# Router logits with the padded weights stationary: one change to a hybrid attention and mixture-of-experts block

## The chip, the cores and the metric

The kernel runs on one core of a Trainium2 chip. The metric is the device time of one execution in microseconds (us); the kernel before was timed three times. Engines: PE is TensorE's matmul, PEld its weight load, DVE VectorE, ACT ScalarE, POOL GpSimd, SP SyncE, which here only issues DMAs. Each engine works through its own instructions in order.

## The reference

One decoder block on 512 tokens of width 1024, all float32. The part that the change touches comes after attention:

```python
x = x + (gate_p * pool_out + gate_a * attn_out) @ w_out[l]
hn = rmsnorm(x, norm2_g[l]).reshape(B * S, D)
x = x + hier_moe(hn, w_router_group[l], b_router_group[l], ...)
# inside hier_moe
pg = softmax(hn @ w_rg + b_rg)          # 4 groups, the best one is taken
le = hn @ w_re + b_re                   # 32 experts, 8 in each group
# top 2 of the chosen group's 8 experts; every token goes through those two
```

The router's logits are thus 36 numbers for each token: 4 group logits and 32 expert logits, a contraction over 1024 channels. All 32 experts have tokens, and each has three float32 matrices of 2 MB (gate, up, down).

## The kernel before, in words

The 512 tokens are four tiles of 128 (NT = 4). The first third computes the input projection, pooling, attention and the branch projections. Then `out_proj` (L777) multiplies the merged branches by w_out, chooses experts and gathers the rows of the first pair of experts; then a loop over 16 pairs of experts (L1087) does their gate, up and down projections and adds the results to the tokens. The schedule is written out by hand: the order of the instructions of each engine is the order in which the program issues them.

**The order in `out_proj`.** `tok_unit` (L266) issues 12 matmuls for one tile, half the channels and 512 output columns; `mid` names functions that it calls after its inner steps k = 0 to 3. After each unit `tick()` (L450) runs the tasks that `after(n, ...)` (L460) has set for then, in the order in which they were set. The second half of the columns takes eight units in the order (0,0) (1,0) (0,1) (2,0) (1,1) (3,0) (2,1) (3,1), each pair being (tile, half of the channels). When a tile's second unit is done, `x2_half` (L648) adds the residual on DVE (L650) and sums squares on ACT (L653), and `x2_rstd` (L655) makes the mean on DVE (L658, L659) and its inverse root on POOL. Tiles 0 and 1 then go on so: in the next unit the second half of the tile is transposed (`rt_transpose`, PE L680, copied out by ACT L681); after that unit come `norm2` (ACT L670), `store_rows` (a DMA from POOL's queue, L673), `rt_logits` (PE L690) and `rt_select` (twelve DVE instructions, L695 to L726, that end with the choice `A_b`); after the unit behind it comes `ranked` (L771), which counts on PE how many earlier tokens chose each expert (L739, L740) and makes R1 and P on DVE. Tile 2 does its logits inside the last unit. Tile 3 does them behind it, between the matmuls (L850) that gather the first pair's rows.

**The logits.** For each tile and each of 8 blocks of 128 channels, the transposed tokens are the stationary operand (128 x 128) and the router weights `wr` (128 x 36) move. A float32 matmul counts as two matmul instructions in the trace, so a tile's logits are 16.

**Buffers and loads.** Weights come through a pool of 23 buffers of 8 KB a partition (NBIG = 23), and so do the activations. `prefetch` (L614) puts loads of expert weights into SP's queue. A load waits there until its buffer is free, and the loads behind it wait too.

Of the kernel before, what the change touches and what calls it, by code (L numbers as in the profile page):

```python
# [10 lines left out]
F32 = mybir.dt.float32  # L11
# [6 lines left out]
OP = mybir.AluOpType  # L18
# [4 lines left out]
NT, ND = SEQ // 128, D // 128  # L23
# [3 lines left out]
NG, EPG, NE = 4, 8, 32  # L27
DE = 512
CAP = 64
# [19 lines left out]
def hybrid_block_kernel(  # L49
# [27 lines left out]
    nc = tc.nc  # L77
# [5 lines left out]
    const = ctx.enter_context(tc.tile_pool(name="const", bufs=1))  # L83
# [12 lines left out]
    def T(name="t"):  # L96
        return sm.tile([128, 512], F32, tag="T", name=f"{name}{next(names)}")
# [90 lines left out]
    lam_v = T("lam_v")[:, :4 * HD].rearrange("p (i d) -> p i d", i=4)  # L188
    cols = const.tile([128, 8], F32, name="cols")
    wgrp = T("wgrp")[:, :512].rearrange("p (g d) -> p g d", g=4)  # L190
    wr = const.tile([128, ND, NG + NE], F32, name="wr")
    br = const.tile([128, NG + NE], F32, name="br")

    for i, g in enumerate((q_norm_g, k_norm_g)):
# [8 lines left out]
    nc.sync.dma_start(cols[:, 4:5], bass.AP(tensor=subln_g.tensor, offset=subln_g.offset, ap=[[1, 128], [1, 1]]))  # L203
    nc.sync.dma_start(wgrp, pool_w[0].rearrange("g c d -> c g d"))
    nc.sync.dma_start(wr[:, :, :NG], w_rg[0].rearrange("(c p) n -> p c n", p=128))
    nc.sync.dma_start(wr[:, :, NG:], w_re[0].rearrange("(c p) n -> p c n", p=128))
    g2c = const.tile([128, ND], F32, name="g2c")
    g2p = const.tile([128, ND], F32, name="g2p")
    nc.sync.dma_start(g2p, bass.AP(tensor=norm2_g.tensor, offset=norm2_g.offset, ap=[[ND, 128], [1, ND]]))
# [14 lines left out]
    def late_consts():  # L224
        for h in range(H):
            ts(bias4[:, h, :], dist, -(2.0 ** (-8.0 * (h + 1) / H)), None, op0=OP.mult)
        nc.vector.reciprocal(rc, rc)
        nc.vector.tensor_copy(ident_h, ident)
        tt(wr, wr, g2c[:, :, None].to_broadcast([128, ND, NG + NE]), op=OP.mult)
        ts(qk_g[:, 0:1], qk_g[:, 0:1], HD ** -0.5, None, op0=OP.mult)  # L230
        ts(cols[:, 4:5], cols[:, 4:5], 1.0 - LAM_INIT, None, op0=OP.mult)
        lsum = const.tile([128, 2], F32, name="lsum")
        lscr = T("lscr")[:, :HD]
        for i in range(2):
            stt(lscr, lam_v[:, 2 * i, :], 1.0, lam_v[:, 2 * i + 1, :], op0=OP.mult, op1=OP.mult,
                accum_out=lsum[:, i:i + 1])
        nc.scalar.activation(lsum, lsum, AF.Exp)
        stt(neglam, lsum[:, 1:2], -LAM_INIT, lsum[:, 0:1], op0=OP.add, op1=OP.subtract)
# [221 lines left out]
    def after(n, fn):  # L460
        tasks.append((unit_no[0] + n, fn))
# [183 lines left out]
    sel = {}  # L645
# [20 lines left out]
    def norm2(t):  # L666

        if t == 0:
            xn2.extend(S([128, 2, ND, 128], name="xn2") for _ in range(2))
        nc.scalar.mul(xn2_tile(t), acc_t(t).rearrange("p (q j) -> p j q", j=ND), sel[t]["r"])  # L670
# [4 lines left out]
    def rt_transpose(t, hf):  # L675
        sel[t]["T", hf] = T("xgT")[:, :512].rearrange("p (j q) -> p j q", j=4)
        p = bank("th", (128, 4, 128))
        for j in range(4):
            c = hf * 4 + j
            nc.tensor.transpose(p[:, j, :], acc_t(t)[:, c * 128:(c + 1) * 128], ident)  # L680
        nc.scalar.copy(sel[t]["T", hf], p)  # L681

    def rt_logits(t, *halves):
        if t in (0, NT - 1) and 0 in halves:
            first["lg", t] = bank("lg", (128, NT, 128))
        q = sel[t]
        q["lg"] = first["lg", NT - 1 if t == NT - 1 else 0][:, t]
        for hf in halves:
            for j in range(4 * hf, 4 * hf + 4):
                mm(q["lg"][:, :NG + NE], q["T", hf][:, j % 4, :], wr[:, j, :], start=j == 0, stop=j == ND - 1)  # L690

    def select_ops(t):
        q = sel[t]
        lg = small([128, NG + NE], "lg", bufs=4)
        stt(lg, q["lg"][:, :NG + NE], q["r"], br, op0=OP.mult, op1=OP.add)  # L695
        yield
        mg = small([128, 1], "mg", bufs=4)
        nc.vector.tensor_reduce(mg, lg[:, :NG], axis=AX.X, op=OP.max)
        yield
        cand = small([128, NG], "cand")  # L700
        best = small([128, 1], "best")
        stt(cand, lg[:, :NG], mg, iota_g, op0=OP.is_equal, op1=OP.mult)
        yield
        nc.vector.tensor_reduce(best, cand, axis=AX.X, op=OP.max)
        yield
        pen = small([128, NG], "pen")
        ts(pen, iota_g, best, NEG, op0=OP.not_equal, op1=OP.mult)
        yield
        le = small([128, NG, EPG], "le", bufs=4)
        tt(le, lg[:, NG:].rearrange("p (g e) -> p g e", e=EPG), pen[:, :, None].to_broadcast([128, NG, EPG]),  # L710
           op=OP.add)
        yield
        le = le.rearrange("p g e -> p (g e)")
        top = small([128, 8], "top", bufs=4)
        nc.vector.max(top, le)
        yield
        idx = small([128, 8], "idx", U32)
        nc.vector.max_index(idx, top, le)
        yield
        idf = small([128, 2], "idf", bufs=4)  # L720
        nc.vector.tensor_copy(idf, idx[:, 0:2])
        yield
        o1 = small([128, NE], "o1", bufs=4)
        ts(o1, iota_u, idf[:, 0:1], None, op0=OP.is_equal)
        yield
        stt(A_b[:, t, :], iota_u, idf[:, 1:2], o1, op0=OP.is_equal, op1=OP.add)  # L726
        yield
        q["v"] = (lg, le, mg, top, idf, o1)

    def rt_select(t, n=None):  # L730
        if "ops" not in sel[t]:
            sel[t]["ops"] = select_ops(t)
        for _ in itertools.islice(sel[t]["ops"], n):
            pass

    def rt_rank(t):
        rk = sel[t]["lg"][:, 64:64 + NE]
        for s in range(t):
            mm(rk, ones_b, A_b[:, s, :], start=s == 0, stop=False)  # L739
        mm(rk, tri, A_b[:, t, :], start=t == 0, stop=True)  # L740
        stt(R1[:, t, :], rk, 1.0, A_b[:, t, :], op0=OP.add, op1=OP.mult)
# [35 lines left out]
    def out_proj():  # L777
        i = N_GEMM
        bs = [bank("wo") for _ in range(NT)]
        prefetch(PF[0])  # L780
        for kq in range(2):
            for t in range(NT):
                tok_unit(bs[t], i + kq, kq, t, merged, kq == 0, kq == 1)
                if kq == 1:
                    x2_half(t, 0, bs[t])
                    after(2, lambda t=t: rt_transpose(t, 0))
                tick()
        prefetch(PF[1])
        last = NT - 1
        bs = {}  # L790
        mid = {}
        for n, (t, kq) in enumerate(OUT_ORDER):
            if kq == 0:
                bs[t] = bank("wo")
            tok_unit(bs[t], i + 2 + kq, kq, t, merged, kq == 0, kq == 1, mid)
            mid = {}
            if kq == 1:
                x2_half(t, 1, bs[t])
                if t == last:
                    rt_select(last - 1, 5)  # L800
                x2_rstd(t)
                if t < last - 1:
                    mid = {1: lambda t=t: rt_transpose(t, 1)}
                    after(2, lambda t=t: norm2(t))
                    after(2, lambda t=t: store_rows(t))
                    after(2, lambda t=t: rt_logits(t, 0, 1))
                    after(2, lambda t=t: rt_select(t))
                    after(3, lambda t=t: ranked(t))
                elif t < last:
                    mid = {0: lambda t=t: rt_transpose(t, 1), 1: lambda t=t: rt_logits(t, 0),  # L810
                           2: lambda t=t: (norm2(t), rt_logits(t, 1), rt_select(t, 3))}
            tick()
        prefetch(PF[2])
        assert not tasks, tasks
        rt_logits(last, 0)
        rt_transpose(last, 1)
        gather_first(0, (0,))
        rt_logits(last, 1)
        rt_select(last - 1)
        ranked(last - 1)  # L820
        norm2(last)
        store_rows(last - 1)
        gather_first(0, (1,))
        gather_first(1)
        rt_select(last)
        prefetch(PF[3])
        first["io"] = S([128, 2, D], name="io")
        gather_first(last - 1)
        ranked(last)
        gather_first(last)  # L830
        store_rows(last)
        prefetch(1)
        pairs[0] = first
        for t in range(NT):
            rt_weights(t)
# [7 lines left out]
    def gather_first(t, parts=(0, 1)):  # L843

        if t == 0 and 0 in parts:
            first["b"] = [bank("xg", (128, 4, 128)) for _ in range(2)]
        for i in parts:
            b = first["b"][i]
            for j in range(4):
                mm(b[:, j, :], xn2_tile(t)[:, i * 4 + j, :], first["P"][:, t].rearrange("p e s -> p (e s)"),  # L850
                   start=t + j == 0, stop=t == NT - 1 and j == 3)
        if t == NT - 1:
            first["x"] = x_of(first["b"])
# [327 lines left out]
```

## Time and profile before

| what | value |
|---|---|
| time, median of 3 runs (lowest to highest) | 800.28 us (798.57 to 801.16) |
| the profiled execution: its time, its span | 800.73 us, 798.9 us |
| mean granted TensorE clock | 0.991 |
| PE busy | 771.1 us, 97% of the span |
| DVE, ACT, POOL busy | 361.1, 204.0, 69.2 us |
| moved by DMA | 240.07 MB, mean 301 GB/s |

The span runs from the first to the last instruction; what lies outside it is 1.8 us. A page of the profile shows the span in 40 slices of 20 us: `out_proj` lies in slices 14 to 17, the 16 pairs of experts behind it. Busy time says how long an engine had an instruction in work, not whether it set the end; for that the waits and the DMA queues are read for the same stretch.

### The profile page before, as it was taken

The page shows a single profiled execution, that of the slowest core. Times are in us where ns is not written, and L with a number is a line of the kernel's source. Part 1 is how long each engine was busy: PE and PEld are TensorE (multiplying, and loading weights), DVE is VectorE, ACT ScalarE, POOL GpSimd, SP SyncE. Part 2 cuts the span into 40 slices and gives each one's busy share as a digit, 9 for nine tenths or more (in the row PEclk, how much of TensorE's full clock was granted, in tenths as well). Part 3 has the DMA queues.
Part 4 walks back from the last instruction along what each step waited for, and adds up shares of the span by engine and source line. Part 5 has one row for each costly group of instructions (what it writes and reads, how often), then busy time and mean ns, then how long its engine had stood idle before and what let it go on. Part 6 is the DMA issues. An engine that isn't in the chain of part 4 may idle for free.

```text
span 798.9 us, 9648 instructions
## 1 busy us (share of the span) xinstructions
PE 771.1 (97%) x3686; PEld 450.6 (56%) x3686; DVE 361.1 (45%) x848; ACT 204.0 (26%) x390; POOL 69.2 (9%) x85
## 2 busy tenths in 40 slices
PE   7999999999999999999999999999999999999995
PEld 6888777778888888733444344434444333334343
DVE  5644476545464733662536353335343423324233
ACT  5644445554533433420010001000100000001000
POOL 1131060000100001100010000000000000000000
PEclk9999999999999999989999999999999999999998
DMA  9621013113228782989999999999999999999994
GB/s 326 201 81 53 6 48 106 54 53 106 72 89 313 293 340 91 373 353 425 425 427 427 426 426 426 427 425 426 425 427 426 425 427 425 426 427 426 426 397 146
DMA packets 55711, 240.07 MB, mean 301 GB/s; under 512 B 11176, under 2 KB 14760, under 8 KB 32112
## 3 DMA queue, kind: packets, MB, share of 16 engines
q1 hardware_dynamic: 52928, 233.37, 72.5%
q0 software_dynamic: 2736, 6.07, 1.9%
q8 instruction: 30, 0.49, 0.2%
q14 instruction: 17, 0.14, 0.0%
HBM read 239.13 MB, written 4.19 MB: 305 GB/s over the span
## 4 chain that ended last, share of the span: by engine, by line
PE 70%; DMA 21%; DVE 5%; ACT 2%; issue 1%; SPq 0%; POOL 0%; DVEq 0%; ACTq 0%
PE y L965 9%; PE gate L916 8%; PE up L916 8%; DMA e<-in_w_expert_up_dram 8%; DMA e<-in_w_expert_down_dram 7%; PE g L282 6%; PE g L283 6%; PE g L284 6%; DMA e<-in_w_expert_gate_dram 5%; PE sc L977 5%; PE wo L271 2%; PE wo L273 2%; PE wo L272 2%; PE qk L325 1%; PE o L370 1%; PE v L271 1%
## 5 line engine op out<-in xcount | busy, mean ns | idle before, releaser
L916 PE MATMUL up<-e,io 128*64 128x512 f32 x512 | 119.4, 594 | 9.6 <-DMA e<-in_w_expert_up_dram 9.5
L916 PE MATMUL gate<-e,io 128*64 128x512 f32 x512 | 115.4, 596 | 1.7 <-DVE io L859 1.7
L965 PE MATMUL y<-e,hT 128*64 128x512 f32 x480 | 114.1, 605 | 0.7 <-ACT hT L931 0.7
L922 DVE TENSOR_TENSOR h<-up,sg 128x512 f32<-128x512 f32 x16 | 17.2, 1075 | 183.0 <-PE up L916 183.0
L916 PEld LDWEIGHTS up<-e,io 128*64 128x64 f32 x512 | 38.2, 137 | 87.1 <-issue 67.3
L916 PEld LDWEIGHTS gate<-e,io 128*64 128x64 f32 x512 | 37.9, 137 | 69.6 <-issue 60.0
L981 DVE TENSOR_TENSOR acc<-sc,acc 128x512 f32<-128x512 f32 x124 | 76.8, 683 | 0.2
L965 PEld LDWEIGHTS y<-e,hT 128*64 128x64 f32 x480 | 35.4, 139 | 69.0 <-issue 62.8
L157 DVE SCALAR_TENSOR_TENSOR wl<-w,g1c,wh 128x512 fp32r<-128x512 f32 x64 | 49.0, 792 | 38.6 <-ACT wh L156 38.5
L282 PE MATMUL g<-hTh,wh 128*128 128x512 f32 x160 | 64.8, 405 | 0.1
L283 PE MATMUL g<-hTl,wh 128*128 128x512 f32 x160 | 62.4, 390 | 0.0
L284 PE MATMUL g<-hTh,wl 128*128 128x512 f32 x160 | 62.4, 390 | 0.0
L971 DVE SCALAR_TENSOR_TENSOR yl<-y,wv,yh 128x512 fp32r<-128x512 f32 x31 | 23.3, 751 | 76.1 <-ACT yh L970 76.1
L977 PE MATMUL sc<-yh,PT 128*128 128x512 f32 x124 | 53.3, 430 | 0.0
L970 ACT ACTIVATE yh<-y,wv 128x512 fp32r<-128x512 f32 x31 | 21.3, 688 | 118.0 <-PE y L965 113.8
L977 PE MATMUL sc<-yl,PT 128*128 128x512 f32 x124 | 48.9, 394 | 0.0
L931 ACT COPY hT<-ht 128x512 f32<-128x512 f32 x16 | 9.4, 587 | 145.7 <-PE ht L929 145.7
L156 ACT ACTIVATE wh<-w,g1c 128x512 fp32r<-128x512 f32 x64 | 44.6, 720 | 0.9 <-DMA w<-in_w_in_dram 0.9
L872 POOL MEMSET io<- 128x1024 f32 x15 | 14.3, 952 | 335.7 <-PE xg L882 335.7
L920 ACT ACTIVATE sg<-gate 128x512 f32<-128x512 f32 x16 | 9.6, 597 | 130.5 <-PE gate L916 130.5
L977 PEld LDWEIGHTS sc<-yh,PT 128*128 128x128 f32 x124 | 23.3, 188 | 28.1 <-issue 24.7
L282 PEld LDWEIGHTS g<-hTh,wh 128*128 128x128 f32 x160 | 30.0, 188 | 13.1 <-issue 5.4
(227 smaller groups left out, 1089.3 us busy)
## 6 DMA issues: line engine op xcount, KB each, us to landing
e<-in_w_expert_gate_dram SPq DMA_DIRECT2D x64, 1024.0 KB, 19.7
e<-in_w_expert_down_dram SPq DMA_DIRECT2D x62, 1024.0 KB, 19.6
e<-in_w_expert_up_dram SPq DMA_DIRECT2D x60, 1024.0 KB, 20.2
w<-in_w_in_dram SPq DMA_DIRECT2D x16, 1024.0 KB, 5.6
w<-in_w_out_dram SPq DMA_DIRECT2D x4, 1024.0 KB, 6.0
e<-in_w_expert_up_dram SPq DMA_DIRECT2D x8, 512.0 KB, 14.1
x<-in_x_dram SPq DMA_DIRECT2D x4, 512.0 KB, 6.2
w<-in_w_pool_up_dram SPq DMA_DIRECT2D x2, 1024.0 KB, 4.9
```

Source lines behind the costliest of these rows:

```text
L156: nc.scalar.mul(hi, src, g)
L157: stt(lo, src, g, f(hi), op0=OP.mult, op1=OP.subtract)
L271: mm(b, ahi[:, k, s], whi[:, k, :], start=first and k == 0, stop=False)
L282: mm(b, whi[:, k, s], ahi[:, k, :], start=first and k == 0, stop=False)
L283: mm(b, whi[:, k, s], alo[:, k, :], start=False, stop=False)
L284: mm(b, wlo[:, k, s], ahi[:, k, :], start=False, stop=last and k == 3)
L916: mm(b[s, :], xs[par][:, j, :], w[par][:, k, :], start=j == 0, stop=j == 7)
L965: mm(y[r, :], hTt[:, j, r], w[j // 2][par][:, j % 2, hf * 512:(hf + 1) * 512], start=j == 0, stop=j == 3)
L970: nc.scalar.mul(hi, y, wv)
L971: stt(lo, y, wv, f(hi), op0=OP.mult, op1=OP.subtract)
L977: mm(b, PT[:, t * 128:(t + 1) * 128], y2[k], start=k == 0, stop=k == 1)
L981: tt(a, b, a, op=OP.add)
```

## The change

The router weights are padded with zeros from 36 to 64 columns (CAP = 64) and become the stationary operand; the transposed tokens (128 columns) move. The even blocks of channels are summed on partitions 0 to 63 of a PSUM tile, the odd ones on partitions 64 to 127, so that `lgT` holds two half sums of the transposed logits. ACT copies `lgT` to SBUF (`sT`), and one matmul with `sT` stationary and a constant `fold` (two identities added, 128 x 36) moving adds the halves and transposes them back. For tiles 0 and 1 the logits are put ahead of `norm2`, and `rt_fold` and `rt_select` run a unit later than the logits, ahead of `ranked`. For tile 2 the logits' second half is put ahead of `norm2`, and the fold and the first three instructions of the selection move from step 2 to step 3 of the last unit. For tile 3 the fold stands between two gathers. The start gains a memset of `wr` on POOL and one addition on DVE.

```diff
-    wr = const.tile([128, ND, NG + NE], F32, name="wr")
+    wr = const.tile([128, ND, CAP], F32, name="wr")
+    fold = const.tile([128, NG + NE], F32, name="fold")
+    nc.gpsimd.memset(wr, 0.0)
...
-        tt(wr, wr, g2c[:, :, None].to_broadcast([128, ND, NG + NE]), op=OP.mult)
+        tt(wr, wr, g2c[:, :, None].to_broadcast([128, ND, CAP]), op=OP.mult)
+        tt(fold, ident[:, :NG + NE], ident[:, CAP:CAP + NG + NE], op=OP.add)
...
     def rt_logits(t, *halves):
+        last = t == NT - 1
...
-        q["lg"] = first["lg", NT - 1 if t == NT - 1 else 0][:, t]
+        b = first["lg", NT - 1 if last else 0]
+        q["lgT"] = b[:, t]
+        q["lg"] = b[:, 0, :NG + NE] if last else b[:, NT - 1, t * (NG + NE):(t + 1) * (NG + NE)]
         for hf in halves:
             for j in range(4 * hf, 4 * hf + 4):
-                mm(q["lg"][:, :NG + NE], q["T", hf][:, j % 4, :], wr[:, j, :], start=j == 0, stop=j == ND - 1)
+                s = slice(j % 2 * CAP, (j % 2 + 1) * CAP)
+                mm(q["lgT"][s], wr[:, j, :], q["T", hf][:, j % 4, :], start=j < 2, stop=j >= ND - 2)
+        if 1 in halves:
+            q["sT"] = T("lgT")[:, :128]
+            nc.scalar.copy(q["sT"], q["lgT"])
+
+    def rt_fold(t):
+        mm(sel[t]["lg"], sel[t]["sT"], fold, start=True, stop=True)
...
                     mid = {1: lambda t=t: rt_transpose(t, 1)}
+                    after(2, lambda t=t: rt_logits(t, 0, 1))
                     after(2, lambda t=t: norm2(t))
                     after(2, lambda t=t: store_rows(t))
-                    after(2, lambda t=t: rt_logits(t, 0, 1))
-                    after(2, lambda t=t: rt_select(t))
+                    after(3, lambda t=t: rt_fold(t))
+                    after(3, lambda t=t: rt_select(t))
                     after(3, lambda t=t: ranked(t))
                 elif t < last:
                     mid = {0: lambda t=t: rt_transpose(t, 1), 1: lambda t=t: rt_logits(t, 0),
-                           2: lambda t=t: (norm2(t), rt_logits(t, 1), rt_select(t, 3))}
+                           2: lambda t=t: (rt_logits(t, 1), norm2(t)), 3: lambda t=t: (rt_fold(t), rt_select(t, 3))}
...
         gather_first(0, (1,))
+        rt_fold(last)
         gather_first(1)
         rt_select(last)
```

## Rows read from the trace of the kernel before

**Rows 1.** Waits in SP's queue, 240 to 420 us: waiter, cause, total us, times, longest
```profile
SPq L620 <- PE wo L273: 42.9, 4, 20.2
SPq L620 <- DMA xn_rows<-xn: 10.1, 1, 10.1
```
**Rows 2.** Table by stretch: from:to and length in us, granted clock, DMA share, GB/s
```profile
300.00:309.00 9.00, 1.00 0.00 0
309.00:315.00 6.00, 1.00 0.22 89
...
340.00:344.00 4.00, 1.00 0.44 117
...
400.00:760.00 360.00, 1.00 1.01 426
```
**Rows 3.** SP in order of time: start us, us, instruction
```profile
314.79 0.33 SPq L620 DMA_DIRECT2D e<-in_w_expert_gate_dram  x1
324.78 0.33 SPq L620 DMA_DIRECT2D e<-in_w_expert_gate_dram  x1
341.71 0.33 SPq L620 DMA_DIRECT2D e<-in_w_expert_up_dram  x1
```
**Rows 4.** The chain of waits: start us, us, work (x instructions)
```profile
305.12 0.44 PE th L680 x4
306.95 1.71 PE lg L690 x16
354.46 9.12 PE y L965 x32
385.62 7.02 PE y L965 x32
```
**Rows 5.** ACT in order of time: a copy from PSUM, a small activation
```profile
305.65 0.59 ACT L681 COPY xgT<-th 128x512 f32<-128x512 f32 x1 [0.34 <-PE th L680]
336.45 0.30 ACT L751 ACTIVATE ex<-lg,nm 128x4 f32<-128x4 f32 x1 [5.28 <-DVE nm L746]
```
**Rows 6.** PE in order of time around the ranks of tiles 0 and 1
```profile
311.10 0.39 PE L273 MATMUL wo<-wh,ml 128*128 128x512 f32 x1
311.50 0.18 PE L740 MATMUL lg<-A_b,tri 128*128 128x32 bf16 x1
...
319.12 0.39 PE L273 MATMUL wo<-wh,ml 128*128 128x512 f32 x1
```
**Rows 7.** DVE in order of time, tiles 0 to 3
```profile
308.76 0.25 DVE L695 SCALAR_TENSOR_TENSOR lg<-lg,r,br 128x36 f32<-128x36 f32 x1 [3.07 <-PE lg L690]
...
311.19 0.25 DVE L726 SCALAR_TENSOR_TENSOR A_b<-iota_u,idf,o 128x32 bf16<-128x32 f32 x1
311.52 0.69 DVE L650 TENSOR_TENSOR acc<-wo,acc 128x512 f32<-128x512 f32 x1
...
313.26 0.15 DVE L659 TENSOR_SCALAR ms<-ms 128x1 f32<-128x1 f32 x1
...
321.23 0.15 DVE L659 TENSOR_SCALAR ms<-ms 128x1 f32<-128x1 f32 x1
...
325.02 0.69 DVE L650 TENSOR_TENSOR acc<-wo,acc 128x512 f32<-128x512 f32 x1
```
**Rows 8.** PE by stretch: length, busy time (x instructions), granted clock, DMA share, GB/s
```profile
349.50:351.50 2.00, 1.78 (x12) 1.00 0.99 418
...
354.50:358.50 4.00, 4.00 (x10) 0.50 1.01 428
...
366.50:368.00 1.50, 0.00 (x0) 1.00 1.04 437
```
**Rows 9.** PE in order of time: first matmuls of full width behind column halves
```profile
363.46 0.50 PE L977 MATMUL sc<-yh,PT 128*128 128x512 f32 x1
363.80 0.40 PE L977 MATMUL sc<-yl,PT 128*128 128x512 f32 x1
364.03 0.39 PE L977 MATMUL sc<-yh,PT 128*128 128x512 f32 x1
```

More of the change, by code (lines that the diff above doesn't have):

```diff
@@ L205, in hybrid_block_kernel @@
     nc.sync.dma_start(wr[:, :, :NG], w_rg[0].rearrange("(c p) n -> p c n", p=128))
-    nc.sync.dma_start(wr[:, :, NG:], w_re[0].rearrange("(c p) n -> p c n", p=128))
+    nc.sync.dma_start(wr[:, :, NG:NG + NE], w_re[0].rearrange("(c p) n -> p c n", p=128))
     g2c = const.tile([128, ND], F32, name="g2c")
@@ L694, in select_ops @@
         lg = small([128, NG + NE], "lg", bufs=4)
-        stt(lg, q["lg"][:, :NG + NE], q["r"], br, op0=OP.mult, op1=OP.add)
+        stt(lg, q["lg"], q["r"], br, op0=OP.mult, op1=OP.add)
         yield
@@ L736, in rt_rank @@
     def rt_rank(t):
-        rk = sel[t]["lg"][:, 64:64 + NE]
+        rk = sel[t]["lgT"][:, 64:64 + NE]
         for s in range(t):
```

## The prediction

> **What bounds the kernel now.** I read SP's waits first, because the last stage moves 12.6 MB of weights for each pair of experts, then the DMA table by stretch, then SP, PE and DVE in order of time between 300 and 345 us.
>
> The table [rows 2] splits the end of the kernel in two. From 400 to 760 us the DMA engines are full (share 1.01, 426 GB/s): there the loads set the pace and PE can't shorten anything. Before that there is a hole: no transfer at all from 300 to 309 us, a share of 0.22 to 315 us, and 0.44 between 340 and 344 us. The waits in SP's queue [rows 1] say what the hole waits for: 42.9 us on the matmuls of w_out (L273), 10.1 us on the store of the normed rows. In order of time [rows 3], one group of expert loads leaves at 314.79, behind the unit (3,0); the next at 324.78, behind the last unit (3,1); the one at 341.71 waits for tile 3's store to land. So `out_proj` is where PE still sets the end: its matmuls free the buffers, the loads wait for the buffers, and from 344 us on the rest is bytes at a fixed rate. A delay of PE between 300 and 335 us is a delay of the loads, hence of the end. A delay of PE behind 345 us costs little.
>
> **What the change removes on PE.** A tile's logits take 1.71 us for 16 instructions [rows 4], 0.107 us each, though only 36 columns move. In the new form 128 columns move and the blocks alternate between two column halves. The nearest row is the down projection, which alternates halves the same way: 7.02 us for 32 instructions of 512 columns [rows 4], 0.219 each; a quarter of it is 0.055, and 16 take 0.88 us. The other end, without overlap between halves, is the transposes' 0.44 us for four of 128 columns [rows 4], 0.11 each, 1.76 us for 16. I take 0.88, since the code has the form of the former. The gain is 0.83 us a tile (at worst -0.05).
>
> **What it adds.** A fold of two instructions of 36 columns with a full stationary operand costs what two of the old logits cost, 0.21 us; it lies between that and about 0.6, if PE waits for ACT's copy. The copy of 128x128 lies between a small activation, 0.30, and a copy of 128x512, 0.59 us [rows 5]: about 0.37. For tiles 0 and 1 a whole unit of 12 matmuls covers it. For tile 2 three matmuls do, about 0.69 us against the copy and two handovers of some 0.06 each; without that cover it costs up to 0.5. `norm2` and the store now queue behind the copy on ACT; for tiles 0 and 1 nobody reads them until the gathers, some 10 us later. The memset of `wr`, its multiplication (512 columns instead of 288, so 224/512 of the 0.69 us that DVE's addition of that size takes [rows 7], 0.3) and the addition for `fold` lie at the start, among constants that PE needs only behind 300 us. I take them as nothing; if DVE's splitting of weights behind them made PE wait, they would cost up to 1 us.
>
> At each change between full width and column halves there may be a price. Behind a block of column halves the first full-width matmul starts 0.34 us before its successor instead of 0.23 [rows 9]: 0.11 us. Six blocks of logits make 12 changes, 1.3 us at most; the sum leaves them out, since most lie beside waits, and the range holds them. The Trainium skill, "TensorEngine Tiling (Array Packing)", section Key Properties, says that a change of the tiling mode drains TensorE. By that rule, if nothing of a 0.39 us matmul stayed covered, 12 changes would take 12 x 0.39 = 4.7 us (an estimate) and the time would be 815.2. The trace agrees that there is a price, and puts it at 0.11.
>
> **What it moves, which decides.** For tiles 0 and 1 the selection used to be issued one unit ahead of the rank. While DVE chose, PE did the 12 matmuls of the next unit: the choice was ready at 311.19 + 0.25 = 311.44, the unit's last matmul ended at 311.10 + 0.39 = 311.49, and the rank started at 311.50 [rows 6, 7]. PE waited for nothing. Now fold, selection and rank are tasks of the same tick, behind the unit (1,1) for tile 0 and behind (2,1) for tile 1. Three queues meet there:
> - DVE has `x2_half` and `x2_rstd` of the next tile ahead of the selection. The addition starts at 311.52, ACT sums the squares, and the second instruction on the mean ends at 313.26 + 0.15 = 313.41 [rows 7].
> - Only then come the twelve instructions of the selection, 308.76 to 311.44 before, 2.68 us: 316.09, and 316.15 with the 0.06 to the rank.
> - On PE the rank stands right behind the fold, and behind the rank the whole next unit, the transposes and the logits of the next tile. All wait. SP's loads wait for that unit.
>
> So PE stands still from 311.49 to 316.15 but for the fold: 4.66 us later for tile 0. For tile 1 the same from 319.12 + 0.39 = 319.51 [rows 6] to 321.23 + 0.15 + 2.68 + 0.06 = 324.12 [rows 7]: 4.61. The two folds lie inside.
>
> For tiles 2 and 3: fold and three of the twelve instructions of the selection now stand behind the last unit and ahead of tile 3's addition (325.02 [rows 7]), on which tile 3's transposes wait. Fold with its handover, 0.3, and 3/12 of 2.68 us make them 1.0 us later; the shorter logits vanish in that wait. The last rank keeps this 1.0.
>
> **The sum.** At the loads behind the last unit (324.78): 4.66 + 4.61 - 3 x 0.83 (tiles 0, 1, 2) = 6.8 us later. At tile 3's store and the first gate matmuls: 7.8. The loads resume for good between the two: 7.3.
>
> **The clock.** PE will be idle twice for about 4.5 us. The nearest rows [rows 8]: from 349.5 to 354.5 us PE had little work (twelve narrow matmuls, then gaps), the granted clock fell from 1.00 (2.4 GHz) to 0.50 (1.2 GHz) and was still there from 354.5 to 358.5, so the down projection took 9.12 instead of 7.02 us [rows 4], 2.1 us lost. In the idle stretch 366.5 to 368 the clock held. A stall is nearer the former. It costs between 0 and 2.1; I take 1.5 each, a little less than the row since the stall is shorter, 3.0 together. It lies ahead of the loads, so it counts.
>
> Sum: +7.3 + 3.0 = 10.3. The profiled execution took 800.73 (span 798.9 and 1.8 outside), which gives 811.0; the median of the runs is 0.45 lower, so 810.5.
>
> **The rivals.**
> - The clock holds in both stalls: for it, 366.5 to 368 us; against it, that this gap was a third as long. 800.3 + 7.3 = 807.6.
> - The loads cover it (not slower): SP's groups turn out to have other buffers in time, the hole doesn't grow, and at 426 GB/s the end stays at 800.3. For it: full DMA from 344 us on, and PE that catches up there. It decides if the stretches without transfers between 300 and 345 us add up to no more than now, about 16 us; against it, the loads at 314.79 and 324.78 leave as the matmuls end. If only the 2.2 us of idle between 340 and 344 are absorbed, 808.3.
> - The stall doesn't come, since DVE has the choice ready when the unit ends (say the selection gets ahead of the addition). Then PE gains 3 x 0.83, pays 2 x 0.21 and tile 3's 1.0: -1.1, 799.2. It decides if the wait for the rank is under 1 us. Against it: both orders are written out.
>
> **How the numbers follow.** Forecast with the clock falling 0.62, clock holds 0.22, loads cover it 0.08, no stall 0.08. The two slower cases with their bounds reach from 804.9 (clock at 1.00, loads 6.8 us late, 2.2 of idle absorbed: 800.3 + 4.6) to 814.8 (7.8 late, 4.2 for the clock, and 3 x 0.83 if the shorter logits gain nothing). The range, 803.5 to 815, takes these in and leaves out little more than the 0.16 of the other two. Runs of this kernel spread by 0.3%, 2.4 us, so less is no change: slower 0.84 from the first two, no change 0.13 and faster 0.03 from the last two, which lie near 800 and 799.
>
> **What would show it.** Right: PE idle for over 4 us ahead of the first rank (L740) and again ahead of tile 1's (L739), each released by DVE's `A_b` (L726 before); the selection of tile 0 behind the mean of tile 1; logits of 0.9 us; the load that left at 324.78 leaving at 331 to 335; PE's clock at 0.50 behind a stall; 426 GB/s behind that as now. Wrong: ranks without a wait, logits near 1.7 us, or a hole in the DMA table no longer than now.

## The result, and the profile after

The changed kernel takes 820.23 us (819.29 to 820.97, 4 runs), the one before 800.39 beside it; the ratio is 1.0246, 95% interval 1.0233 to 1.0259, or 19.7 us slower. The forecast was 810.5, within 803.5 to 815. The direction and the waits were right; about half of the loss was missing.

What the page of the changed kernel says of the whole (busy time, then GB/s in 40 slices of 20.5 us):

```profile
span 818.8 us, 9678 instructions
PE 776.9 (95%) x3694; PEld 452.2 (55%) x3694; DVE 361.2 (44%) x849; ACT 205.0 (25%) x394; POOL 69.7 (9%) x86
GB/s 317 221 56 52 47 6 103 103 1 153 54 138 298 351 190 123 262 349 418 418 420 418 418 418 417 421 418 419 418 421 418 415 420 418 418 422 418 418 383 149
```

PE is busy 5.8 us more in a span 19.9 us longer, so most of the loss is waiting. The table by stretch (length, granted clock, DMA share, GB/s) answers to [rows 2]:

```profile
300.00:309.00 9.00, 1.00 0.00 0
309.00:315.00 6.00, 0.90 0.21 87
315.00:325.00 10.00, 0.72 0.29 93
325.00:340.00 15.00, 0.77 0.64 229
340.00:344.00 4.00, 1.00 1.02 408
344.00:400.00 56.00, 0.94 0.96 388
400.00:760.00 360.00, 1.00 1.01 419
```

and the kernel before in the stretch that [rows 2] leaves out:

```profile
315.00:325.00 10.00, 1.00 0.93 337
```

Two things are to be seen. The hole in the transfers is longer: the share between 315 and 325 us is 0.29, where it was 0.93. And in the last line, where the DMA engines are full (1.01) in both kernels, they move 419 GB/s and not 426. Nothing in the forecast spoke of that.

SP in order of time, the loads that answer to [rows 3]:

```profile
321.13 0.33 SPq L623 DMA_DIRECT2D e<-in_w_expert_gate_dram  x1
336.74 0.33 SPq L623 DMA_DIRECT2D e<-in_w_expert_gate_dram  x1
353.71 0.33 SPq L623 DMA_DIRECT2D e<-in_w_expert_up_dram  x1
```

They leave 6.3, 12.0 and 12.0 us later than before. The second was forecast for 331 to 335 us and leaves at 336.74. PE in order of time (start us, us, instruction, idle time before it and its cause), answering to [rows 6]:

```profile
306.53 0.39 PE L276 MATMUL wo<-wh,ml 128*128 128x512 f32 x1
306.85 1.09 PE L698 MATMUL lg<-xgT,wr 128*64 128x128 f32 x16
307.87 0.50 PE L274 MATMUL wo<-wh,mh 128*128 128x512 f32 x1
308.21 0.40 PE L275 MATMUL wo<-wl,mh 128*128 128x512 f32 x1
...
310.52 0.39 PE L276 MATMUL wo<-wh,ml 128*128 128x512 f32 x1
310.75 0.30 PE L704 MATMUL lg<-fold,lgT 128*128 128x36 f32 x2
315.49 0.19 PE L754 MATMUL lg<-A_b,tri 128*128 128x32 bf16 x1 [4.44 <-DVE A_b L740]
315.52 0.77 PE L274 MATMUL wo<-wh,mh 128*128 128x512 f32 x1
...
321.26 1.09 PE L698 MATMUL lg<-xgT,wr 128*64 128x128 f32 x16
...
324.92 0.39 PE L276 MATMUL wo<-wh,ml 128*128 128x512 f32 x1
325.15 0.30 PE L704 MATMUL lg<-fold,lgT 128*128 128x36 f32 x2
327.47 0.19 PE L753 MATMUL lg<-A_b,ones_b 128*128 128x32 bf16 x1 [2.01 <-DVE lg L709]
329.89 0.19 PE L754 MATMUL lg<-A_b,tri 128*128 128x32 bf16 x1 [2.24 <-DVE A_b L740]
329.92 0.77 PE L274 MATMUL wo<-wh,mh 128*128 128x512 f32 x1
...
334.49 0.50 PE L274 MATMUL wo<-wh,mh 128*128 128x512 f32 x1
```

Both ranks wait for `A_b`: 4.44 us for tile 0. Tile 1's wait comes in two parts: its first instruction, which needs only tile 0's choice, waits 2.01 us for DVE's read of the logits, which lie in the same PSUM tile, the second 2.24 us for its own choice. DVE in order of time shows why, answering to [rows 7]:

```profile
310.95 0.69 DVE L653 TENSOR_TENSOR acc<-wo,acc 128x512 f32<-128x512 f32 x1 [5.30 <-PE wo L276]
312.49 0.16 DVE L661 TENSOR_TENSOR ms<-ss 128x1 f32<-128x1 f32 x1 [0.85 <-ACT sq L656]
312.68 0.15 DVE L662 TENSOR_SCALAR ms<-ms 128x1 f32<-128x1 f32 x1
312.76 0.26 DVE L709 SCALAR_TENSOR_TENSOR lg<-lg,r,br 128x36 f32<-128x36 f32 x1
...
315.19 0.25 DVE L740 SCALAR_TENSOR_TENSOR A_b<-iota_u,idf,o 128x32 bf16<-128x32 f32 x1
```

Tile 0's selection stands behind tile 1's addition and mean, though ACT had copied its logits out from 308.05 on. The chain of waits shows what the new logits of tiles 0 and 1 take, against 1.71 us in [rows 4]:

```profile
306.92 1.02 PE lg L698 x16
...
321.33 1.02 PE lg L698 x16
```

### The profile page after: what moved, and what is told of

Same layout as the page of the kernel before. It is cut to its first block, busy times and chain, and to the rows that moved or that the text cites. A ratio compares the mean times of both kernels' runs of the same rounds, so it can differ in the third digit from the quotient of the medians.

```text
span 818.8 us, 9678 instructions
## 1 busy us (share of the span) xinstructions
PE 776.9 (95%) x3694; PEld 452.2 (55%) x3694; DVE 361.2 (44%) x849; ACT 205.0 (25%) x394; POOL 69.7 (9%) x86
## 4 chain that ended last, share of the span: by engine, by line
PE 64%; DMA 26%; DVE 5%; ACT 2%; issue 1%; SPq 0%; POOL 0%; DVEq 0%; ACTq 0%
DMA e<-in_w_expert_down_dram 10%; PE y L981 8%; DMA e<-in_w_expert_gate_dram 8%; DMA e<-in_w_expert_up_dram 8%; PE gate L932 7%; PE up L932 7%; PE g L285 6%; PE g L286 6%; PE g L287 6%; PE sc L993 4%; PE wo L274 2%; PE wo L276 2%; PE wo L275 2%; PE qk L328 1%; PE o L373 1%; PE v L274 1%
## 5 line engine op out<-in xcount | busy, mean ns | idle before, releaser
L932 PE MATMUL up<-e,io 128*64 128x512 f32 x512 | 121.1, 595 | 13.2 <-DMA e<-in_w_expert_up_dram 13.2
## 6 DMA issues: line engine op xcount, KB each, us to landing
e<-in_w_expert_down_dram SPq DMA_DIRECT2D x62, 1024.0 KB, 19.9
```

Of the source, the lines that this page charges most:

```text
L932: mm(b[s, :], xs[par][:, j, :], w[par][:, k, :], start=j == 0, stop=j == 7)
```

## The experiments

The theory formed on these traces has two parts. *Order*: fold, selection and rank in one tick make PE wait, and the clock falls in the wait. *Address*: 426 became 419 GB/s because of where the large buffers lie. `wr` grew by 896 bytes a partition and `fold` adds 144, which takes 160; the pool of 23 buffers comes after them in SBUF and moved from 22784, a multiple of 256, to 23840, 32 bytes behind one. No trace shows these starts: the steps between them follow from the sizes in the edits, and what the runs below show is which steps cost time. The rival to the second part: the slower loads are a sequel of the later, differently bunched start. Times are medians, ratios are to the kernel before on the same chip; the experiments ran on three chips, so they are compared by their ratios.

**Only the address, 32, 64, 128 and 256 bytes.** The kernel before, with one small constant tile made longer; it is allocated ahead of the large buffers and its new part is not used:

```diff
-    offs = const.tile([128, NOV], F32, name="offs")
+    offs = const.tile([128, NOV + 8], F32, name="offs")[:, :NOV]    # + 16, + 32, + 64
```

> The kernel before with nothing changed but one constant tile 32 bytes a partition longer, so that the pool of 23 large buffers starts 32 bytes behind a multiple of 256 bytes (22816 instead of 22784), as it does in the changed kernel (23840). Theory (address): the changed kernel's loads run at 419 instead of 426 GB/s because its buffers no longer start at a multiple of 256 bytes; here too 418 to 420 GB/s from 400 to 760 us and 460 x 7/426 = 7.6 us more, 808. Rival (sequel of the stalls): the slower loads come from the later, differently bunched start; here 426 GB/s and 800.4.

> As the run with 32 bytes, but 128 bytes, so that the large buffers start at 22912, a multiple of 128 and not of 256. Address theory with a grain of 256 bytes: 808 as with 32. With a grain of 128 or less: 800.4 and 426 GB/s. Rival (sequel of the stalls): 800.4.

> As the run with 256 bytes, but 64 bytes: the large buffers start at 22848, a multiple of 64 and not of 128 or 256. Theory (256 bytes is the grain): 419 to 420 GB/s and 807 to 808, as with 32 and 128. Rival (64 bytes is enough and the 128 bytes of the earlier run stood badly for another reason): 800.

> The kernel before with the same constant tile longer by 256 bytes, so that the large buffers start at 23040, again a multiple of 256. Theory (only the place within 256 bytes counts): 426 GB/s and 800. Rival (any move of the buffers costs, or a longer tile does): 807 to 808 as with 32 and 128 bytes.

| start of the large buffers | past a multiple of 256 by | time, us | ratio (95%) |
|---|---|---|---|
| 22816 | 32 | 808.33 | 1.0101 (1.0065 to 1.0137) |
| 22848 | 64 | 807.84 | 1.0095 (1.0067 to 1.0124) |
| 22912 | 128 | 806.92 | 1.0081 (1.0055 to 1.0106) |
| 23040 | 0 | 800.22 | 1.0009 (0.9994 to 1.0024) |

The same line of the table by stretch, with 32 bytes:

```profile
400.00:760.00 360.00, 1.00 1.01 419
```

with 128 bytes:

```profile
400.00:760.00 360.00, 1.00 1.01 420
```

with 256 bytes:

```profile
400.00:760.00 360.00, 1.00 1.01 426
```

No instruction differs between these kernels. A start 32 bytes past a multiple of 256 costs as much as one 64 or 128 bytes past it, 6.5 to 8.1 us by the ratios (2 to 3 to each side) and 1.4 to 1.6% of the rate; a whole 256 bytes cost nothing. That settles the address against the sequel of the stalls, which are not in these kernels, and against a cost of any move. The Trainium skill, "DMA: Bandwidth & Descriptors", section How a descriptor splits into AXI transactions, says that a transaction must start at a multiple of 256 bytes: when a descriptor doesn't, its first transaction starts at the multiple below, and the bytes ahead of the descriptor's start are fetched without use and still cost. The page speaks of reading and gives no time. These runs agree that 256 bytes is the grain, for buffers that are written. That the page's mechanism is the cause here is not shown: the loss doesn't grow with the bytes ahead of the start, 32, 64 or 128.

**The changed kernel with its buffers at a multiple of 256.**

```diff
-    offs = const.tile([128, NOV], F32, name="offs")
+    offs = const.tile([128, NOV + 56], F32, name="offs")[:, :NOV]
```

> The changed kernel with one constant tile 224 bytes a partition longer, so that its large buffers start at 24064, a multiple of 256. Address theory: 426 GB/s again and 820.2 - 7.6 = 812.6, of which 12 us remain for stalls and clock, as PE's gather of the last tile is 12.9 us later than in the kernel before. Rival (sequel of the stalls): 419 GB/s and 820.

Measured 813.28, ratio 1.0157 (1.0127 to 1.0188), 12.6 us over the kernel before. Its table has

```profile
400.00:760.00 360.00, 1.00 1.01 426
```

So 7.1 us of the 19.7 are the address, and 12.6 the order with all that hangs on it. Each of the two is known to some 2.5 us to each side.

**Only the order.** The kernel before, addresses and logits untouched:

```diff
-                    after(2, lambda t=t: rt_select(t))
+                    after(3, lambda t=t: rt_select(t))
```

> The kernel before with one word changed: the selection of tiles 0 and 1 is set for after(3) instead of after(2), so that it meets the rank in one tick as in the changed kernel; logits, fold and addresses are those of before. Theory (order): PE waits 4.6 us ahead of each of the two ranks, the clock falls in both and costs about 2 each: 800.4 + 9.3 + 4 = 813 to 814, at 426 GB/s. Rival (the fold and the copy are what PE waits for): no wait at the ranks and 800.4 to 801.

Measured 813.86, ratio 1.0182 (1.0143 to 1.0221). PE's waits, 4.6 at tile 0 and the rest at tile 1 (waiter, cause, total us, times, longest):

```profile
PE lg L740 <- DVE A_b L726: 6.8, 2, 4.6
PE lg L739 <- DVE lg L695: 2.1, 1, 2.1
```

One word of the schedule, without fold, copy or new logits, does what the change did. That it takes some 2 us more than the change with its buffers put right fits the longer logits, but lies within the two intervals.

**The clock by itself.** The changed kernel at a multiple of 256, with PE kept at work through the wait:

```diff
+    def hold():
+        hb = bank("hold", (128, 4, 128))
+        for j in range(20):
+            mm(hb[:, j % 4, :], ident, ident, start=True, stop=True)
...
-                    after(3, lambda t=t: rt_fold(t))
+                    after(3, lambda t=t: (rt_fold(t), hold()))
```

> The changed kernel with its buffers at a multiple of 256 bytes and its waits as they are, but with 20 multiplications of the identity (40 instructions of 0.11 us, 4.4 us) on PE between fold and rank of tiles 0 and 1, so that PE works through the wait; their result is not used. Theory (the clock has a price of its own, 2.4 us a stall): the granted clock stays at 1.00 from 309 to 340 us and the time is 813 - 4.7 = 808 to 809. Rival (the clock's fall hides behind another wait): 812 to 813.

Measured 808.05, ratio 1.0098 (1.0077 to 1.0118). PE by stretch in the changed kernel (length, busy time and instructions, granted clock, DMA share, GB/s): the two waits, and what PE did behind each,

```profile
311.50:315.40 3.90, 0.00 (x0) 0.79 0.33 134
315.50:320.30 4.80, 4.80 (x14) 0.50 0.00 0
320.50:325.00 4.50, 4.50 (x32) 0.99 0.64 208
326.00:329.80 3.80, 0.19 (x1) 0.69 1.02 363
330.00:333.50 3.50, 3.50 (x11) 0.50 0.63 259
```

and with PE kept at work:

```profile
311.50:315.40 3.90, 3.90 (x38) 1.00 0.34 139
315.50:320.30 4.80, 4.80 (x36) 1.00 0.15 29
...
326.00:329.80 3.80, 3.80 (x31) 1.00 0.98 346
330.00:333.50 3.50, 3.39 (x30) 1.00 0.04 9
```

In the changed kernel the clock fell from 1.00 (2.4 GHz) to 0.50 (1.2 GHz) within each wait, and was still there for the first 4 to 5 us of work behind it. With work in the wait it stayed at 1.00. The same pieces of work in that run, from the first matmul behind the rank to tile 1's logits, and to the first matmul behind half of tile 2's logits:

```profile
315.57 0.47 PE L274 MATMUL wo<-wh,mh 128*128 128x512 f32 x1
318.97 1.09 PE L698 MATMUL lg<-xgT,wr 128*64 128x128 f32 x16
...
327.63 0.47 PE L274 MATMUL wo<-wh,mh 128*128 128x512 f32 x1
330.22 0.50 PE L274 MATMUL wo<-wh,mh 128*128 128x512 f32 x1
332.27 0.39 PE L276 MATMUL wo<-wh,ml 128*128 128x512 f32 x1
```

They take 3.40 and 2.59 us; in the changed kernel they take 321.26 - 315.52 = 5.74 and 334.49 - 329.92 = 4.57. So the half clock costs 2.34 and 1.98, 4.3 together. The difference of the ratios, 1.0157 - 1.0098, is 4.7 us, known to some 3 us to each side: the price of the clock reaches the end.

**The rank a unit later.** At a multiple of 256:

```diff
-                    after(3, lambda t=t: ranked(t))
+                    after(4, lambda t=t: ranked(t))
```

> The changed kernel with its buffers at a multiple of 256 bytes again, and the rank of tiles 0 and 1 set one unit later (after(4) instead of after(3)); fold and selection stay where the change put them. Theory (rank behind fold and selection in one tick): both waits of 4.4 us vanish or shrink below 0.5, the clock stays at 1.00, and the logits' gain is left: 3 x 0.69 - 3 x 0.23 for the folds - about 1.0 at tile 3, so 799.5 to 801. Rival (the fold itself or ACT's copy is the wait): 810 and more.

Measured 801.29, ratio 1.0012 (1.0002 to 1.0022). Tile 0's rank still waits 1.1 us, more than the 0.5 expected: the task set first runs first, so the rank stands ahead of tile 1's logits in its tick. The clock stays at 1.00.

**Fold and selection in the next unit, the rank behind it.**

```diff
+        later = {}
...
-            mid = {}
+            mid = later.pop(n + 1, {})
...
-                    after(3, lambda t=t: rt_fold(t))
-                    after(3, lambda t=t: rt_select(t))
-                    after(3, lambda t=t: ranked(t))
+                    later[n + 2] = {0: lambda t=t: (rt_fold(t), rt_select(t))}
+                    after(4, lambda t=t: ranked(t))
```

> The changed kernel with its buffers at a multiple of 256 bytes, fold and selection of tiles 0 and 1 in the first step of the next unit, ahead of the next tile's addition on DVE, and the rank a unit later. Theory: no wait at the ranks, DVE's addition at most 0.9 us later, time 799.3 to 800.5, within a few tenths of the run with only the rank moved; against the kernel before a gain of at most 1 us, since the logits gain only 0.69 us a tile and the fold takes 0.23 back. If the logits' gain reached the loads whole: 798.5.

> The same order as in the run that puts fold and selection into the next unit, but with the buffers where the change puts them, 32 bytes behind a multiple of 256. Theory (address and order add up): 807.5 (7.6 us more), 419 GB/s from 400 to 760 us. Rival (the slower loads need the stalls too): 800.

At a multiple of 256: 800.81, ratio 1.0001 (0.9989 to 1.0012), a little above what was expected. With the buffers where the change puts them: 809.47, ratio 1.0112 (1.0097 to 1.0127), and

```profile
400.00:760.00 360.00, 1.00 1.01 419
```

So the new logits, put in without harm, gain nothing that can be measured; 0.60 a tile was to be had, against folds and a later tile 3. The address costs 8.9 us here without a stall (7 to 11 by the intervals). No version here beats the kernel before.

## Why the prediction was wrong

- **The bound.** Right: the loads that wait for PE in `out_proj` carry its delay to the end. They left 12.0 us later, and the kernel with its buffers put right is 12.6 us slower. The forecast for these loads was 6.8 + 3.0 = 9.8 us; the 2.2 us between are the logits and the clock, below.
- **The waits at the ranks, which decided.** Right in place, cause and size. From the start of the unit's last matmul to the rank it was 311.50 - 311.10 = 0.40 us for tile 0 [rows 6]; it is 315.49 - 310.52 = 4.97: 4.57 more, forecast 4.66. For tile 1 the trace gives 4.55 from that matmul to the next unit, forecast 4.61. The experiment on the order alone shows the cause.
- **The logits.** Mis-sized. The forecast was 0.88 us a tile from the down projection; they take 307.87 - 306.85 = 1.02. The change of mode, left out of the sum, costs about what the forecast named: the logits start 0.32 us behind the w_out matmul ahead of them, where it was 0.23, and the first full-width matmul behind them starts 0.34 us before its successor, where it was 0.31. From w_out matmul to w_out matmul tile 0 gains 0.60, not 0.83.
- **The fold and the copy.** Right within its bounds: 0.30 and 0.27 us, forecast 0.21 (up to 0.6) and 0.37, both under cover for tiles 0 and 1. Tile 3's transposes waited 1.0 us as forecast. The memset and the addition at the start cost nothing that is left at the logits: the w_out matmul ahead of them starts at 306.53, before at 306.55.
- **The clock.** Right that it falls in both waits, mis-sized: 3.0 us forecast, 2.34 + 1.98 = 4.3 by the traces. The forecast took the row of 2.1 us as the upper bound and shaved it, since these waits are shorter than that stretch; the half clock behind them still lasted 4 to 5 us of full work.
- **The step that failed.** "From 344 us on the rest is bytes at a fixed rate." The sum had no term for the stretch in which the DMA engines are full, and the forecast named "426 GB/s behind that as now" as a sign that it was right. The rate fell to 419, because the larger `wr` and the new `fold` moved every large buffer off a multiple of 256 bytes. The larger `wr` was costed as a memset and a multiplication, at the start; that it lies ahead of the buffers in SBUF was not looked at. By the three ways to separate it (the change with and without the padding, the kernel before with 32 bytes, and the order without a stall at both addresses) it is 7.1, 8.1 and 8.9 us, which agree within their intervals.

The ledger of PE up to the loads: 4.57 + 4.55 for the waits, 2.34 + 1.98 for the clock, less what the logits of tiles 0 to 2 gain (starts of matmuls in each pair of times). For tile 0, from the w_out matmul ahead of its logits to the last ahead of its rank, that is 306.55 to 311.10 in the kernel before against 306.53 to 310.52 here: 0.56. For tiles 1 and 2 the run with PE kept at work has it at the full clock. From the first matmul behind tile 0's rank to the last ahead of tile 1's it is 311.52 to 319.12 before against 315.57 to 322.62, 0.55; from the first behind tile 1's rank to the last of w_out it is 319.57 to 324.59 against 327.63 to 332.27, 0.38. That makes 11.95, and the loads show 11.96. The forecast of 3 x 0.83 for the logits was 1.0 too high, that for the clock 1.3 too low. With 7 to 9 for the address the 19.7 are reached. Had the rate held, the time would have been 813, as the run with the padding shows, and within the range.

## What to carry to other kernels

Where the end of a kernel is a stretch of full DMA, look at everything that a change does to the addresses of the buffers that it fills: a constant that grows by a few bytes ahead of them cost 1% of this kernel, and putting padding behind it brings that back. When a helper is moved to a later tick, look for what else runs in that tick and on which engines in order: a producer and its consumer in one tick have lost the work that stood between them. Waits of PE like these two, 4.6 us each, are to be priced with the slower clock behind them, here about half of the wait again.

## What was not expected of the hardware

The loads' rate depends on the start of the buffer in SBUF: 426 GB/s at 22784, 23040 and 24064, 419 to 420 at 32, 64 or 128 bytes past a multiple of 256, with the same transfers and a DMA share of 1.01 in each. The share alone would not have shown it; the bytes beside it did.
